# A hybrid attention and recurrence block: two operand slots of the recurrence, and the place of one transposition

## The chip, the cores and the metric

The kernel runs on one core of a Trainium2 chip. The metric is the device time of one execution in microseconds (us). The core has a matrix engine (TensorE, PE in the profile), a vector engine (VectorE, DVE), a scalar engine (ScalarE, ACT), a general engine (GpSimd, POOL) and an engine that here only issues transfers (SyncE, SP). Each works through its own list of instructions; semaphores tie the lists together.

## The reference

One transformer block over a sequence of 1024 tokens and a width of 1024: a projection `w_in` into queries, keys and values of an attention with forget gates (8 heads of 64), into the inputs of an RWKV7 recurrence (8 heads of 64) and into two gates; both branches, their gated sum through `w_o`, and then a convolutional feed-forward part with 2816 channels. The change lies in the recurrence:

```python
def rwkv7_time_mix(p, mu, w0, w2, a0, a2, g2, k_k, k_a, r_k, ln_w, ln_b):
    p = p + (token_shift(p) - p) * mu
    r, k, v, xw, xa, xg = _split(p, RWKV_SPLITS)
    ...
    kk = heads(k * k_k)
    kk = kk / jnp.maximum(jnp.sqrt(jnp.sum(kk * kk, axis=-1, keepdims=True)), L2_EPS)
    k_mod = k.astype(jnp.float32) * (1 + (a - 1) * k_a)
    ...
    def step(state, inp):
        r_t, w_t, k_t, v_t, a_t, b_t = inp
        sa = jnp.einsum('bhvk,bhk->bhv', state, a_t)
        state = state * w_t[:, :, None, :] + sa[..., None] * b_t[:, :, None, :] + v_t[..., None] * k_t[:, :, None, :]
        y_t = jnp.einsum('bhvk,bhk->bhv', state, r_t)
        return state, y_t
    ...
    bonus = (jnp.sum(r_h * k_h * r_k, axis=-1, keepdims=True) * v_h).reshape(bsz, seq, RWKV_WIDTH)
    return ((y + bonus) * g).astype(p.dtype)
```

The last two lines but one hold the bonus: a sum over the 64 channels of each head, times v.

## The kernel before, in words

**Stages.** The program modulates and normalises the input, computes the projections, runs the recurrence with part of the projections between its steps, then the attention, the two output projections, and the feed-forward part. A float32 matmul with the full number of digits is made of three products of rounded parts ("hi" and "lo"): `load_w` loads a block of weights into `raw`, ACT rounds it to hi (line 272), DVE computes lo = raw - hi (line 274).

**The recurrence** works on 8 units: 4 pairs of heads p by 2 halves hf of the sequence, named p_hf (0_0, 0_1, 1_0 and so on to 3_1). A unit has 8 chunks of 64 tokens. In each unit `pre` (from line 697) does what needs no state, and `main` (from line 831) does the rest.

- `pre` loads the log decays into `cum` (line 711) and the rates into `al` (line 713), sums the decays along the chunks with a scan on DVE (line 715, in place), makes `el` and `en` from it with exponentials on ACT (lines 719 and 721), normalises the keys (`ksq`, `rn`, `kr`, lines 723 to 732), forms `ar` and `bk` (lines 737 to 744) and the product `rkb` for the bonus (line 748, in the slot of ksq). Matmuls give the chunk matrices `E` (line 764). Corner blocks of 32 by 32 go to memory and back in another layout (lines 772 and 776), a loop of 31 steps of two small DVE instructions inverts them (lines 784 and 786), and the result returns through memory to `TT` (lines 789 and 797). The transposed v and a are copied to `UV` and `QA` (ACT line 810, DVE line 811), and `q` follows. Then come the bonus sums: `head_sums` (line 825, the function at lines 690 to 696), which rounds its input to a part hi (ACT, line 692), forms the rest lo on POOL (line 693) and adds both over the heads' channels with two matmuls. `bon` (line 827) is the product with v.
- `main` transposes the corner of TT into `X` on DVE (line 842), goes through `xi`, `X` (ACT, line 852), `zi` and back to `TT` (ACT, line 859), `uw`, `mz`, and then a chain through the 8 chunks: a matmul with the state on PE, a scaled copy of it to `S` on ACT (line 903). The normalisation of the output `y` with two more head sums follows (lines 915 to 937).

**Slots.** Most intermediate tiles come from a pool `rw` with one buffer for each tag; `tmp("cum")` takes the buffer tagged cum of width 512 and waits until the tile that had it before has been read for the last time. A tag is used for several tiles in a unit: `ksq` for the squares, for rn, and for rkb; before the change `cum` and `en` are taken again by the two parts of the bonus sums.

**The order.** PE's order is written out by hand: `Weave` (line 48) runs `main` of one unit and `pre` of a later one as two chains of generators, and wherever a chain yields a wait it fills PE with steps of the projections (`rkv_items`, `qk_steps`, `v_steps`, `gate_steps`), by a model of matmul times. The projections leave PSUM through two buffers tagged `big`: `shifted` (lines 354 to 369) scales one copy on ACT (line 366) and evacuates the bank on DVE (line 369); `qk_steps` rounds queries and keys (lines 393 and 395). The orders of DVE, ACT, POOL and SP in this part are chosen by the compiler's scheduler from the dependences and its own costs, except for extra dependences given by hand. Such a dependence of class NOSYNC makes no wait on the chip; it only puts one instruction behind another in a list. `marks` holds instructions for it: the transposition of line 842 goes behind the last `S` copy and the last `E` product recorded at that point.

Of the kernel before, what the change touches and what calls it, by code (L numbers as in the profile page):

```python
# [10 lines left out]
F32R = mybir.dt.float32r  # L11
AF = mybir.ActivationFunctionType
ALU = mybir.AluOpType
# [3 lines left out]
S = 1024  # L17
KT = 8
NH = 512
# [113 lines left out]
def hybrid_block(ctx: ExitStack, tc: tile.TileContext, a, out):  # L133
# [4 lines left out]
    def mm(o, lhsT, rhs, start, stop, more=False):  # L138

        weave.mm_cost(o, lhsT, rhs)  # L140
        nc.tensor.matmul(o, lhsT, rhs, start=start, stop=stop, skip_group_check=more)  # L141
# [5 lines left out]
    def f32(ap):  # L147
        return ap.bitcast(F32)

    tt, stt, ts = nc.vector.tensor_tensor, nc.vector.scalar_tensor_tensor, nc.vector.tensor_scalar  # L150
# [15 lines left out]
    def V(name, i=0, n=1):  # L166
        o, _ = VEC[name]
        return vec[:, o + i : o + i + n]
# [13 lines left out]
    omu = cp.tile([128, 14], F32, name="omu")  # L182
# [61 lines left out]
    marks = {}  # L244
# [40 lines left out]
    def gemm_steps(ps, w, x, cs, nk=KT, w0=0, by_kt=False):  # L285
        (wh, wl), (xh, xl) = w, x
        order = [(i, kt) for i in range(3) for kt in range(nk)]
        if by_kt:
            order.sort(key=lambda o: o[1])
        for n, (i, kt) in enumerate(order):  # L290
            ww, xx = ((wh, xh), (wh, xl), (wl, xh))[i]
            k0 = (w0 + kt) * 128
            mm(ps, ww[:, k0 : k0 + 128], xx[:, kt, cs], start=n == 0, stop=n == len(order) - 1)
            yield
# [51 lines left out]
    with ExitStack() as es:  # L346
# [4 lines left out]
        def big(name):  # L351
            return pb.tile([128, NH], F32, tag="big", name=name)

        def gen(name):
            return pr.tile([128, NH], F32, tag="gen", name=name)

        def shifted(w, ti, hf, dst, prev, name, by_kt=False):

            ps = big(f"ps_{name}{hf}")
            yield from gemm_steps(ps, w, u, slice(hf * NH, hf * NH + NH), by_kt=by_kt)  # L360
            sh = shp.tile([128, NH + 1], F32, tag="sh", name=f"sh_{name}{hf}")
            if hf == 0:
                nc.vector.memset(sh[:, 0:1], 0.0)
            else:
                nc.vector.tensor_copy(sh[:, 0:1], prev)
            nc.scalar.activation(sh[:, 1 : NH + 1], ps, AF.Copy, scale=V("mu", ti))
            if hf == 0:
                nc.gpsimd.tensor_copy(prev, sh[:, NH : NH + 1])
            stt(dst, ps, omu[:, ti : ti + 1], sh[:, 0:NH], op0=ALU.mult, op1=ALU.add)

        rkv, got, last_col = {}, {}, {}

        def rkv_items(p, hf):
            ts_ = {x: rkp.tile([128, NH], F32, tag=f"{x}{hf}", name=f"{x}{p}{hf}") for x in "rkv"}
            rkv[p, hf], got[p, hf] = [ts_[x] for x in "rkv"], 0

            def steps(w, x, t):
                if hf == 0:
                    last_col[p, x] = shp.tile([128, 1], F32, tag=f"pv{x}", name=f"pv{p}{x}")
                yield from shifted(w, t, hf, ts_[x], last_col[p, x], f"rkv{t}")  # L380
                got[p, hf] += 1

            for x, t in (("k", 4 + p), ("r", p), ("v", 8 + p)):
                yield (lambda t=t: w_in(12 + t)), (lambda w, x=x, t=t: steps(w, x, t))
# [305 lines left out]
        def head_sums(ps, x, hi, lo):  # L690

            nc.scalar.copy(hi, x)
            nc.gpsimd.tensor_tensor(lo, x, f32(hi), op=ALU.subtract)
            yield 3400
            mm(ps, blk_r, hi, start=True, stop=False)
            mm(ps, blk_r, lo, start=False, stop=True)

        def pre(k, p, hf):
# [5 lines left out]
            def tmp(nm, w=NH, bufs=1, dt=F32):  # L704
                return rw.tile([128, w], dt, tag=nm, name=f"{nm}{n}", bufs=bufs)

            def chunk_tile(nm, bufs, *dims):
                return rw.tile([128, *dims], F32, tag=nm, name=f"{nm}{n}", bufs=bufs)

            cum = tmp("cum")  # L710
            nc.sync.dma_start(cum, d_lora[0, p, :, cs])
            al = tmp("al")
            nc.sync.dma_start(al, d_lora[1, p, :, cs])
            for c0 in (0, 256):
                nc.vector.tensor_tensor_scan(cum[:, c0 : c0 + 256], cst2[:, 128:384], cum[:, c0 : c0 + 256], initial=0.0,
                                             op0=ALU.mult, op1=ALU.add)
# [3 lines left out]
            en = tmp("en")  # L720
# [10 lines left out]
            kr = tmp("kr")  # L731
# [15 lines left out]
            rkb = tmp("ksq")  # L747
# [6 lines left out]
            E = chunk_tile("E", 2, NCU, 2, 3, CH)  # L754
            QA = chunk_tile("QA", 2, NCU, 2, CH)
            UV = chunk_tile("UV", 2, NCU, 2, CH)
            for c0 in range(0, NCU, 4):
                ps = [gen(f"p1_{n}{h}{c0}") for h in range(2)]
# [54 lines left out]
            ps = [gen(f"tb{n}{h}") for h in range(2)]  # L813
# [8 lines left out]
                    mm(q[HS[h], c * CH : c * CH + CH], E[HS[1 - h], c, h, 0, :], UV[HS[1 - h], c, h, :], start=True, stop=True)  # L822
            nc.vector.tensor_copy(QA[:, :, 0, :], c3(q))
            bp = gen(f"bs{n}")
            yield from head_sums(bp, rkb, tmp("cum", dt=F32R), tmp("en", dt=F32R))
            bon = tmp("bon", bufs=2)
            tt(bon, bp, vv, op=ALU.mult)
            units[p, hf] = dict(ready=ready, pcd=pcd, ar=ar, E=E, QA=QA, TT=TT, bon=bon, UV=UV)
# [1 line left out]
        def main(k, p, hf):  # L830
# [3 lines left out]
            pcd, ar, E, QA, TT, bon, UV = (o[k] for k in ("pcd", "ar", "E", "QA", "TT", "bon", "UV"))  # L834
# [5 lines left out]
            yield max(0, o["ready"] - weave.now - 2500)  # L840
            for h in range(2):
                i = nc.vector.transpose(X[B0[h], :, :], TT[B0[h], :, 0:32])
                for x in ("S", "E"):
                    if x in marks:
                        tc.add_manual_dep(i.ins, marks[x].ins.name, NOSYNC)
            yield max(1300, o["ready"] - weave.now)
# [16 lines left out]
            for c0 in range(0, NCU, 4):  # L863
                ps = gen(f"uw{n}{c0}")
                for c in range(c0, c0 + 4):
                    for h in range(2):
                        x = (c - c0) * 128
# [7 lines left out]
            for c0 in range(0, NCU, 4):  # L875
                ps = gen(f"mz{n}{c0}")
                for c in range(c0, c0 + 4):
                    for h in range(2):
                        x = (c - c0) * 128
# [9 lines left out]
            S = [state.get(p)]  # L889
# [76 lines left out]
        def pre_chain():  # L966
            for k, (p, hf) in enumerate(order):
                while got[p, hf] < 3:
                    yield 200
                yield from pre(k, p, hf)  # L970
                if p < 3:
                    weave.first.extend(rkv_items(p + 1, hf))
                yield 0

        def main_chain():
            for k, (p, hf) in enumerate(order):
                while (p, hf) not in units:
                    yield 200
                yield from main(k, p, hf)
                yield 0  # L980
# [205 lines left out]
    def bank(k, name):  # L1186
        return pb.tile([128, NH], F32, tag="big", name=name) if k > 5 else pz.tile([128, NH], F32, tag=f"p{k}", name=name)
# [125 lines left out]
    for x in range(2):  # L1313
        for n in range(8):
            if x or n:
                k = 8 * x + n + 1
# [313 lines left out]
    ps = {t: [bank(k, f"wo{t}_{c}") for c, k in enumerate(ks)] for t, ks in enumerate(((0, 5), (6, 7), (1, 2)))}  # L1630
# [12 lines left out]
    def wo_do(t, k):  # L1643
        ps = [bank(k + c, f"wo{t}_{c}") for c in range(2)]
        for kt in range(KT):
            wo_mm(t, kt, ps)
        return ps

    ps = wo_do(3, 3)
# [7 lines left out]
    ps = wo_do(4, 0)  # L1657
# [15 lines left out]
    for t, k in ((5, 2), (6, 6), (7, 4)):  # L1673
        ps = wo_do(t, k)
# [229 lines left out]
    for s, k in enumerate(ORDER):  # L1904
        ps = banks[4:] if k in (7, 4, 2) else banks[0:4]
# [109 lines left out]
```

## Time and profile before

| what | value |
|---|---|
| runs, us | 1658.08, 1658.31, 1660.62 (median 1658.31) |
| profiled execution, us | 1662.01 |
| its span, us | 1660.2 |
| mean granted clock of TensorE | 0.989 |
| PE busy, us | 1615.2 (97%) |
| DVE busy, us | 1223.2 (74%) |
| ACT busy, us | 822.3 (50%) |
| POOL busy, us | 130.3 (8%) |
| matmuls | 9694 |

The profile is one execution. A row of the timeline has the start and the duration in us, the engine, the line, the operation, what it writes and reads by the program's names (numbers left out), the shapes, a count of instructions of one kind run together, and in square brackets the idle time of the engine before it with the instruction or transfer that ended this idle time. "SPq" is the issue of a transfer, not the transfer itself. A window's row has the busy us of PE, PE's weight loads, DVE, ACT and POOL, then the granted clock as a share of full speed, the busy share of the transfer engines and the GB/s.

### The profile page before, as it was taken

The numbers are of one execution on the slowest core, as the hardware profiler recorded it, in microseconds if no ns is written. First come the engines' busy times: TensorE is split into PE (matmuls) and PEld (weight loads), VectorE is DVE, ScalarE is ACT, GpSimd is POOL, SyncE is SP. The second block draws the span as 40 slices with busy tenths as digits, with TensorE's granted clock in tenths as the row PEclk, the third lists the DMA queues.
The fourth block names the chain that finished last, engine by engine and source line by source line (L and its number), as shares of the span: only waits on it lengthen the run. The fifth ranks groups of instructions, "written<-read, shape, count | busy, mean of one in ns | idle before, by whom it ended". The sixth has DMA issues, their size and how long they took to land.

```text
span 1660.2 us, 25947 instructions
## 1 busy us (share of the span) xinstructions
PE 1615.2 (97%) x9694; PEld 1346.1 (81%) x9694; DVE 1223.2 (74%) x2371; ACT 822.3 (50%) x1540; POOL 130.3 (8%) x152
## 2 busy tenths in 40 slices
PE   7999999999999999999999999999999999999998
PEld 7777777898978788888778887888888888888886
DVE  5786787878876536888678347897777777786677
ACT  5563335444455656666623225654444444555455
POOL 0011001111111011221022000000000000000000
PEclk9999999999999999999999999999999999999999
DMA  8488645443343246433187411243223223574363
GB/s 336 139 322 238 177 116 140 131 121 97 100 115 97 96 129 153 124 114 110 64 323 265 166 70 58 66 138 108 96 95 120 97 96 108 208 266 156 125 209 108
DMA packets 121645, 240.59 MB, mean 145 GB/s; under 512 B 40048, under 2 KB 48880, under 8 KB 121520
## 3 DMA queue, kind: packets, MB, share of 16 engines
q1 hardware_dynamic: 113040, 220.58, 40.7%
q0 software_dynamic: 8480, 18.37, 4.2%
q8 instruction: 76, 1.25, 0.3%
q14 instruction: 49, 0.40, 0.1%
HBM read 173.35 MB, written 65.54 MB: 144 GB/s over the span
## 4 chain that ended last, share of the span: by engine, by line
PE 62%; DVE 3%; ACT 2%; DMA 1%; issue 1%; SPq 0%; ACTq 0%; DVEq 0%
PE X L141 14%; PE D L141 13%; PE Y L141 7%; PE wo L141 5%; PE br L141 5%; PE gt L141 4%; PE rk_ps L141 4%; PE W L141 3%; PE lg L141 2%; PE ov L141 2%; PE tp L145 2%; DVE nm L1049 1%; DVE P L1059 1%; DMA g<-d_gate 0%; DVE tl L1089 0%
## 5 line engine op out<-in xcount | busy, mean ns | idle before, releaser
L141 PE MATMUL D<-op,op 128*128 128x512 f32 x924 | 209.8, 389 | 0.0
L141 PEld LDWEIGHTS D<-op,op 128*128 128x128 f32 x924 | 173.3, 188 | 36.3 <-DVE op L1252 0.3
L141 PE MATMUL X<-T_m,S 128*128 128x512 f32 x440 | 106.9, 389 | 0.0
L141 PEld LDWEIGHTS X<-T_m,S 128*128 128x128 f32 x440 | 82.5, 188 | 17.5 <-ACT x L1542 0.4
L1251 ACT CAST op<-g 128x512 fp32r<-128x512 f32 x77 | 47.8, 621 | 72.1 <-PE D L141 47.8
L1252 DVE TENSOR_TENSOR op<-g,op 128x512 fp32r<-128x512 f32 x77 | 53.0, 688 | 41.1 <-ACT op L1251 41.1
L1502 DVE SCALAR_TENSOR_TENSOR c<-ab,vec,c 128x512 f32<-128x512 f32 x88 | 65.9, 749 | 18.4 <-ACT c L1505 16.8
L784 DVE TENSOR_TENSOR t<-E,M 128x60 f32<-128x60 f32 (+24 forms) x248 | 56.1, 226 | 26.6 <-DMA M<-sm 20.6
L274 DVE TENSOR_TENSOR lo_in<-raw_in,hi_in 128x512 fp32r<-128x512 f32 x84 | 57.7, 725 | 22.0 <-PE gt L141 7.2
L1466 DVE TENSOR_TENSOR A<-ur,A 128x512 fp32r<-128x512 f32 x64 | 43.9, 688 | 39.0 <-ACT A L1462 38.8
L1466 DVE TENSOR_TENSOR S<-ur,S 128x512 fp32r<-128x512 f32 x66 | 45.5, 691 | 35.2 <-ACT S L1462 35.1
L1462 ACT CAST S<-ur 128x512 fp32r<-128x512 f32 x66 | 41.0, 622 | 56.1 <-DVE ur L1455 30.9
L141 PE MATMUL Y<-T_h,S 128*128 128x512 f32 x264 | 65.6, 398 | 1.6 <-ACT T_h L1720 1.0
L141 PE MATMUL Y<-T_h,A 128*128 128x512 f32 x264 | 63.4, 389 | 0.0
L1053 ACT ACTIVATE P<-lg,nm 128x896 f32<-128x896 f32 (+3 forms) x64 | 47.4, 742 | 29.3 <-DVE nm L1049 19.6
L141 PEld LDWEIGHTS Y<-T_h,S 128*128 128x128 f32 x264 | 50.6, 192 | 13.4 <-ACT T_h L1720 1.8
L1462 ACT CAST A<-ur 128x512 fp32r<-128x512 f32 x64 | 39.6, 621 | 42.9 <-PE X L141 31.0
L141 PE MATMUL W<-B_f,A 128*128 128x512 f32 x252 | 60.6, 389 | 0.0
L786 DVE TENSOR_TENSOR E<-E,t 128x60 f32<-128x60 f32 (+24 forms) x248 | 55.8, 225 | 6.4
L141 PE MATMUL X<-B_b,A 128*128 128x512 f32 x252 | 60.5, 389 | 0.0
L141 PEld LDWEIGHTS Y<-T_h,A 128*128 128x128 f32 x264 | 49.5, 188 | 10.3
L272 ACT CAST hi_in<-raw_in 128x1024 fp32r<-128x1024 f32 x42 | 43.9, 1049 | 25.4 <-PE ps_rkv L141 11.3
(481 smaller groups left out, 4142.0 us busy)
## 6 DMA issues: line engine op xcount, KB each, us to landing
raw_in<-in_w_in SPq DMA_DIRECT2D x50, 512.0 KB, 3.9
wm<-in_w_mod SPq DMA_DIRECT2D x48, 512.0 KB, 6.7
ur<-in_w_up SPq DMA_DIRECT2D x44, 512.0 KB, 4.0
g<-d_g SPq DMA_DIRECT2D x35, 512.0 KB, 3.8
d_g<-gs SPq DMA_DIRECT2D x44, 256.0 KB, 2.0
d_g<-c SPq DMA_DIRECT2D x33, 256.0 KB, 4.3
d_st<-qh SPq DMA_DIRECT2D x64, 128.0 KB, 2.4
stA<-d_st POOLq DMA_DIRECT2D x8, 1024.0 KB, 6.2
```

The costliest lines, as they stand in the source:

```text
L141: nc.tensor.matmul(o, lhsT, rhs, start=start, stop=stop, skip_group_check=more)
L145: nc.tensor.transpose(o, i, eye)
L272: nc.scalar.copy(hi, raw)
L274: nc.vector.tensor_tensor(lo[:, c : c + NH], raw[:, c : c + NH], f32(hi[:, c : c + NH]), op=ALU.subtract)
L784: tt(tv, E32[:, 0:J, s : s + 1].to_broadcast([128, J, W]), M32[:, s : s + 1, s + 1 : 32].to_broadcast([128, J, W]), op=ALU.mult)
L786: tt(E32[:, 0:J, s + 1 : 32], E32[:, 0:J, s + 1 : 32], tv, op=ALU.add)
L1053: nc.scalar.activation(e[:, 0:n], lg[:, 0:n], AF.Exp, bias=nm[:, 0:1], accum_out=nm[:, 1:2])
L1251: nc.scalar.copy(hi, src)
L1252: tt(lo, src, f32(hi), op=ALU.subtract)
L1462: nc.scalar.copy(hi, src)
L1466: tt(lo, src, f32(hi), op=ALU.subtract)
L1502: stt(c, ab[:, x + hf * NH : x + hf * NH + NH], V("conv_w", 22 * x + i), c, op0=ALU.mult, op1=ALU.add)
```

## The change

The bonus sums' two parts are taken from the slots of `kr` and `al` of the same unit in place of `cum` and `en`. And the evacuation of `shifted` (line 369) is recorded as `marks["bank"]`; the transposition of line 842 in the first unit (k == 0) is put behind the last one so recorded, beside S and E.

```diff
@@ -366,7 +366,7 @@
             nc.scalar.activation(sh[:, 1 : NH + 1], ps, AF.Copy, scale=V("mu", ti))
             if hf == 0:
                 nc.gpsimd.tensor_copy(prev, sh[:, NH : NH + 1])
-            stt(dst, ps, omu[:, ti : ti + 1], sh[:, 0:NH], op0=ALU.mult, op1=ALU.add)
+            marks["bank"] = stt(dst, ps, omu[:, ti : ti + 1], sh[:, 0:NH], op0=ALU.mult, op1=ALU.add)
 
         rkv, got, last_col = {}, {}, {}
 
@@ -822,7 +822,7 @@
                     mm(q[HS[h], c * CH : c * CH + CH], E[HS[1 - h], c, h, 0, :], UV[HS[1 - h], c, h, :], start=True, stop=True)
             nc.vector.tensor_copy(QA[:, :, 0, :], c3(q))
             bp = gen(f"bs{n}")
-            yield from head_sums(bp, rkb, tmp("cum", dt=F32R), tmp("en", dt=F32R))
+            yield from head_sums(bp, rkb, tmp("kr", dt=F32R), tmp("al", dt=F32R))
             bon = tmp("bon", bufs=2)
             tt(bon, bp, vv, op=ALU.mult)
             units[p, hf] = dict(ready=ready, pcd=pcd, ar=ar, E=E, QA=QA, TT=TT, bon=bon, UV=UV)
@@ -840,7 +840,7 @@
             yield max(0, o["ready"] - weave.now - 2500)
             for h in range(2):
                 i = nc.vector.transpose(X[B0[h], :, :], TT[B0[h], :, 0:32])
-                for x in ("S", "E"):
+                for x in ("S", "E", "bank") if k == 0 else ("S", "E"):
                     if x in marks:
                         tc.add_manual_dep(i.ins, marks[x].ins.name, NOSYNC)
             yield max(1300, o["ready"] - weave.now)
```

## The prediction

> **What bounds the kernel now.** I read the profile from the whole to the place: first the busy times, then the table of TensorE's waits, then one-microsecond windows and the timeline around the two largest waits near the change.
>
> ```profile
> span 1660.2 us, 25947 instructions
> PE 1615.2 (97%) x9694; PEld 1346.1 (81%) x9694; DVE 1223.2 (74%) x2371; ACT 822.3 (50%) x1540; POOL 130.3 (8%) x152
> ```
>
> PE is busy for 1615.2 of 1660.2 us. Only 45 us are idle, so a change that adds no matmul and removes none can win only what PE waits near it, and the stretches in which PE's clock is low. The profiled execution took 1662.01 us with a span of 1660.2; the runs' median is 1658.31. I sum in the profiled execution's time and carry the difference over to the median. A measurement of this kernel can tell about 0.2% from no change, 3.3 us here: faster means below 1655.0, slower above 1661.6.
>
> The table of PE's waits (line waited at, releaser: us in total, times, longest) has these rows from the recurrence:
>
> ```profile
> PE uw L141 <- ACT TT L859: 2.9, 2, 2.0
> PE qk L141 <- DVE v L369: 2.7, 1, 2.7
> PE v L141 <- DVE vs L955: 1.9, 3, 1.3
> PE br L141 <- DVE mg_m L1306: 1.9, 1, 1.9
> PE sp L141 <- ACT S L903: 1.1, 1, 1.1
> PE qk L141 <- DVE ql L395: 0.7, 1, 0.7
> PE va L141 <- POOL Wts L693: 0.4, 1, 0.4
> ```
>
> (The br row lies after the recurrence; it serves for comparison below.) The eight units together have about 10.7 us of PE waits, and two of them make up 4.8: qk on line 369 and uw on line 859. Both are followed by a low clock. The windows have busy us by engine, then the granted clock, DMA share and GB/s:
>
> ```profile
> 224.00:225.00 1.00, 0.34 (x1) 0.34 (x2) 0.71 (x2) 0.00 (x0) 0.00 (x0) 0.84 0.70 199
> 228.00:229.00 1.00, 1.00 (x20) 0.60 (x20) 0.86 (x5) 1.00 (x3) 0.00 (x0) 0.96 0.00 0
> 286.00:287.00 1.00, 1.00 (x15) 1.00 (x10) 1.00 (x4) 0.24 (x1) 0.00 (x0) 0.56 0.94 381
> 289.00:290.00 1.00, 1.00 (x5) 0.81 (x4) 0.89 (x5) 0.73 (x2) 0.00 (x0) 0.74 0.19 70
> ```
>
> A mean of 0.84 is 0.68 us at full clock and 0.32 at half: the clock halves at 224.68, and 0.96 puts its return at 228.08. In the same way 0.56 and 0.74 give 286.12 to 289.52. Each stretch lasts 3.4 us at half clock and loses 1.7 us of PE's work. The starts are 61.44 us apart, 18 times 3.41, as if the clock were decided on a fixed grid of 3.41 us: then a gap counts by how much of one grid interval it fills.
>
> **First part: the transposition of unit 0_0.** Timeline around the first wait:
>
> ```profile
> 221.75 0.43 DVE L842 STREAM_TRANSPOSE X<-TT 32x256 f32<-32x256 f32 x1 [4.97 <-DMA TT<-se]
> 222.12 1.24 DVE L274 TENSOR_TENSOR lo_in<-raw_in,hi_in 128x512 fp32r<-128x512 f32 x2
> 223.86 0.75 DVE L369 SCALAR_TENSOR_TENSOR v<-ps_rkv,omu,sh_rkv 128x512 f32<-128x512 f32 x1
> 224.66 1.22 PE L141 MATMUL qk<-u_hi,hi_in 128*128 128x512 f32 x2 [2.75 <-DVE v L369]
> 225.06 0.69 DVE L715 TENSOR_TENSOR_SCAN cum<-cst,cum 128x256 f32<-128x256 f32 x1 [0.36 <-DMA cum<-d_lora]
> ```
>
> DVE stands at X for 4.97 us until TT has come from memory. Behind X in its list stand lo_in and the evacuation of v, which frees the PSUM bank for qk. In the changed program's list both stand ahead of X. The evacuation's inputs were long ready, so PE's 2.75 us vanish, and with them the 1.7 us of half clock: 4.45. X itself comes about 0.16 later, and what is late next is the loop of unit 0_1 behind it.
>
> **Second part: other slots.** The number of instructions is unchanged on every engine; the sums' two parts have the same shapes in the new slots. What moves is when slots are free. cum's slot is now free after the en exponential, not after the bonus matmul, so SP takes the next unit's cum load (line 711) some 25 to 80 us sooner, and the scan, el and en move with it: the scans leave the loop stretch of DVE's list, and el and en leave the place ahead of the TT copies for places within the S copies of line 903. al's load (line 713) goes the other way, into cum's former place; line 737 onward needs it only much later. kr now also waits for the bonus matmul, which is always earlier on PE: nothing, as long as PE's order stands (it does).
>
> ```profile
> 281.77 1.27 DVE L715 TENSOR_TENSOR_SCAN cum<-cst,cum 128x256 f32<-128x256 f32 x2 [1.67 <-DMA cum<-d_lora]
> 283.08 0.63 ACT L719 ACTIVATE el<-cum 128x512 f32<-128x512 f32 x1 [4.00 <-DVE cum L715]
> 283.62 0.61 ACT L721 ACTIVATE en<-cum 128x512 f32<-128x512 f32 x1
> 284.14 0.73 ACT L859 COPY TT<-zi 32x256 f32<-32x256 f32 x2
> 284.54 0.43 PE L141 MATMUL uw<-QA,TT 64*64 64x128 f32 x2 [2.05 <-ACT TT L859]
> ```
>
> Here the TT copy waits behind en, en behind el, el 4.00 us for the scan, the scan 1.67 for its load. With scan, el and en gone from ahead of it the copy follows its own matmul zi, and PE gains 2.05 plus the second 1.7: 3.75. The other uw wait goes the same way (0.9), as does va (0.4). Of the 1.9 on vs, which DVE releases, I count 1.1: DVE has a scan of 1.27 less there, but other work in front of it stays. Gains: 4.45 + 3.75 + 0.9 + 0.4 + 1.1 = 10.6.
>
> **What is given back.** First, where the early scans go:
>
> ```profile
> L715 DVE TENSOR_TENSOR_SCAN cum<-cst,cum 128x256 f32<-128x256 f32 x16 | 10.3, 676 | 8.0 <-DMA cum<-d_lora 7.3 <-PE zi L141 0.7
> ```
>
> Sixteen scans stood 7.3 us for their loads. In the first two units loads are still late and the scan now stands ahead of ql (line 395) and of unit 0_0's loop. Between nothing and one scan with its mean stall (1.27 + 1.0 = 2.27) I take 0.75, a stall of that mean less a little cover; the 0.7 wait on ql grows by it.
>
> Second, DVE has little slack after 222 (first the window from 225 to 254):
>
> ```profile
> 225.00:254.00 29.00, 29.00 (x281) 23.38 (x281) 27.00 (x87) 13.08 (x25) 2.11 (x5) 0.95 0.43 116
> ...
> 249.30 0.75 DVE L369 SCALAR_TENSOR_TENSOR k<-ps_rkv,omu,sh_rkv 128x512 f32<-128x512 f32 x1
> 250.94 0.62 PE L141 MATMUL ps_rkv<-u_hi,hi_in 128*128 128x512 f32 x2
> 252.63 0.31 ACT L903 ACTIVATE S<-sp,pcd 128x64 f32<-128x64 f32 x1
> 253.00 0.42 PE L141 MATMUL sp<-S,Mt 128*128 128x64 f32 x2
> ```
>
> PE would come to 250.94 at 247.2 (4.45 less 0.75 earlier). But it needs the bank that k's evacuation frees, and DVE is busy for 27.0 of these 29 us; its list has become shorter only by the scan, its 0.36 stall and some 0.3, less two loop operations put ahead (0.4) and the 0.16: about 1.3. The evacuation ends near 248.75 instead of 250.05, and PE waits some 1.6 to 1.9. Two microseconds on, the S copy stands in ACT's list behind en of unit 1_1, which needs bk's last reader on DVE (line 744); S comes about 0.85 sooner than before, so PE waits another 1.3 at 253.00. Of 3.7 gained, 0.85 is left: 2.85 given back. Bounds: 1 (all cover holds up to 253) and 3.7.
>
> Third, unit 2_0's en stands ahead of the S copy of 300.32:
>
> ```profile
> 299.91 0.69 DVE L744 TENSOR_TENSOR bk<-al,en 128x512 f32<-128x512 f32 x1
> 300.32 0.31 ACT L903 ACTIVATE S<-sp,pcd 128x64 f32<-128x64 f32 x1
> 301.08 0.33 PE L141 MATMUL sp<-S,Mt 128*128 128x64 f32 x2
> ```
>
> en may start only when this bk is written, at 300.60 less the DVE's earliness of some 3.4; en (0.61), the cast behind it and S follow, and the matmul, now 4.6 early, waits about 1.7. Between 0 (bk comes as early as PE) and 3.0. At unit 3_1 the same costs 0.35.
>
> Fourth, unit 2_1's X, at 466.17, now stands ahead of unit 3_0's four QA copies:
>
> ```profile
> 462.52 1.73 DVE L811 COPY QA<-at 64x256 f32<-64x256 f32 x4 [2.32 <-PE at L145]
> 464.04 2.24 SPq L797 DMA_DIRECT2D TT<-se  x4
> 465.36 1.15 PE L141 MATMUL q<-UV,E 64*64 64x64 f32 x32
> 466.17 0.43 DVE L842 STREAM_TRANSPOSE X<-TT 32x256 f32<-32x256 f32 x1 [1.92 <-DMA TT<-se]
> ```
>
> By then all chains are 3.5 early, and TT's loads pass three stores on SP, so X starts near 462.3; with 0.43 of its own and 1.73 of copies the bank of q is free at 464.5. PE stands there at 465.36 - 3.5 = 461.9, hence about 2.4 of waiting; nothing if the bank were free in time, 3.5 at most before all is returned.
>
> Sum: 10.6 - (0.75 + 2.85 + 1.7 + 0.35 + 2.4) = 2.55 gained.
>
> **The clock in the new gaps.** Gaps of 2.75 and 2.05 were each followed by a half-clock stretch; 1.9 (the br row) was not, nor 1.3 on vs. Of the new gaps one (2.4) lies above this border, but its estimate spans it. I count half a stretch, 0.85, with bounds 0 and three stretches, 5.1. Forecast: -2.55 + 0.85 = -1.7; the profiled execution 1660.3, the median 1658.31 - 1.7 = 1656.6.
>
> The Trainium skill, page "TensorE: Matmul & The Clock Gate", section "Why this matters for your kernels", asks for no idle gaps over about 3 us between bursts of matmuls, since one window of idle returns the clock to half. By that rule no new gap costs clock, and the sum would be -2.55, a median of 1655.8. This trace disagrees: gaps of 2.75 and 2.05 were enough.
>
> **The rivals.** *The gain holds*: DVE and ACT keep pace with PE, and the 2.85, 1.7 and 2.4 are hidden; 10.6 - 1.1 = 9.5 at most, with half of these hidden 6 to 8, so about 1651. For it: S chains have fillers between their steps, so a late S need not stop PE. Against it: DVE is 93% busy in the window from 225 to 254, so it can't follow PE there. *Slower, by en ahead of S in every unit*: en waits for line 744, S copies stand behind it on ACT, sp behind them on PE. I find it uncovered at units 1_1, 2_0 and 3_1. Were it so in five more places at 1.7 each, -2.55 + 8.5 = +5.95: 1664.3. It decides from the fourth such place on (-2.55 + 6.8 = +4.25). Against it: before, the whole recurrence shows only one wait on S, of 1.1. *Nothing*: the freed slot isn't used sooner, since SP's order binds the cum load, or later waits swallow all: 1658.3. Against it: the transposition's move alone is firm, and 0.85 of it survives.
>
> **How the numbers follow.** Forecast 0.55 (own range 1653.5 to 1660, from 1.0 to 3.7 in the second term, 0 to 3.0 in the third and 0 to 5.1 of clock, not all at one end); gain holds 0.20; slower 0.15; nothing 0.10. Faster by over 0.2%: 0.38 of the forecast's 0.55 lies below 1655.0, and nearly all of the gain case: 0.21 + 0.19 = 0.40. Slower: 0.13 of the third case and 0.05 of the others: 0.18. Within: 0.42. Range 1651 to 1661.5, which leaves out the far half of the gain case and most of the slower one.
>
> **What would show it.** Right: no wait of qk on line 369 near 222 and full clock there; no uw wait near 282; new PE waits near 251 to 253 on line 369 and S, near 301 on S, near 465 on the QA copies. Wrong: these are absent and the recurrence ends 6 us or more earlier; or S waits appear in most units. I would also be wrong if PE's busy time itself moved by more than the clock explains.

## The result, and the profile after

| comparison | changed, median us | before, median us | ratio to before (95% interval) |
|---|---|---|---|
| the two kernels, 18 runs each | 1655.6 (1650.98 to 1658.38) | 1658.19 (1655.99 to 1664.01) | 0.9980 (0.9971 to 0.9988) |
| changed, second time (e7) | 1655.07 | 1660.48 | 0.9967 (0.9956 to 0.9979) |
| changed, third time (e11) | 1655.02 | 1661.31 | 0.9963 (0.9949 to 0.9976) |

The forecast was 1656.6, a gain of 1.7 us. The kernel is faster by 0.2 to 0.4%: by 2.6 us in the first comparison, at the border between "within 0.2%" and "faster", and by 5.4 and 6.3 us in the two later ones, which lie beyond it. The profiled execution took 1650.98 us, the shortest of the 18, and the profiled one of before, with 1662.01, was longer than all but two of its 18 runs. The two profiles are 11 us apart where the medians are 2.6 apart: what follows takes the places from the profiles and the size from the runs.

The page of the changed kernel, span and busy times:

```profile
span 1649.2 us, 25947 instructions
PE 1607.7 (97%) x9694; PEld 1340.7 (81%) x9694; DVE 1221.3 (74%) x2371; ACT 823.7 (50%) x1540; POOL 128.3 (8%) x152
```

PE's busy time fell by 7.5 us with the same 9694 matmuls, DVE's and ACT's hardly moved. Most of that is clock: ahead of the stretch at the end of the program, which both have, the before profile has nine grid intervals of 3.41 us at half clock, this one five, and four times 1.7 us is 6.8.

PE's waits of 1.8 us and more in the changed kernel, from the recurrence on (line waited at, releaser: total, times, longest):

```profile
PE q L141 <- DVE QA L811: 2.5, 1, 2.5
PE rk_ps L141 <- ACT gm L1163: 2.3, 3, 1.2
PE br L141 <- DVE mg_m L1306: 2.1, 1, 2.1
PE sp L141 <- ACT S L903: 2.0, 3, 1.0
PE ov L141 <- DVE o L1122: 2.0, 1, 2.0
PE br L141 <- ACT hi_br L1214: 1.8, 1, 1.8
PE qk L141 <- DVE ql L395: 1.8, 1, 1.8
```

Gone are qk on line 369 (2.7), uw on line 859 (2.9), v on vs (1.9), va on Wts (0.4). New are q on QA (2.5) and the growth of qk on ql (0.7 to 1.8) and sp on S (1.1 to 2.0). The timeline of the changed kernel at the places that the prediction named, DVE and ACT first:

```profile
219.65 0.74 DVE L369 SCALAR_TENSOR_TENSOR v<-ps_rkv,omu,sh_rkv 128x512 f32<-128x512 f32 x1
221.18 0.43 DVE L842 STREAM_TRANSPOSE X<-TT 32x256 f32<-32x256 f32 x1 [0.78 <-DMA TT<-se]
247.01 0.75 DVE L369 SCALAR_TENSOR_TENSOR k<-ps_rkv,omu,sh_rkv 128x512 f32<-128x512 f32 x1
...
278.20 0.75 ACT L859 COPY TT<-zi 32x256 f32<-32x256 f32 x2 [1.44 <-PE zi L141]
295.45 0.63 ACT L721 ACTIVATE en<-cum 128x512 f32<-128x512 f32 x1 [0.21 <-DVE bk L744]
295.99 0.30 ACT L903 ACTIVATE S<-sp,pcd 128x64 f32<-128x64 f32 x1
...
458.21 0.43 DVE L842 STREAM_TRANSPOSE X<-TT 32x256 f32<-32x256 f32 x1 [5.51 <-DMA TT<-se]
458.58 1.69 DVE L811 COPY QA<-at 64x256 f32<-64x256 f32 x4
```

v's evacuation is done before X; the TT copy at 278.20 follows its own matmul zi instead of an exponential; S at 295.99 stands behind en, which stands behind bk; and the QA copies at 458.58 stand behind an X for which DVE waited 5.51 us. PE at these and a few more places:

```profile
188.74 0.50 PE L141 MATMUL qk<-u_hi,hi_in 128*128 128x512 f32 x1 [1.81 <-DVE ql L395]
195.90 0.61 PE L141 MATMUL ps_rkv<-u_hi,hi_in 128*128 128x512 f32 x2
226.48 0.69 PE L141 MATMUL xi<-X,E 32*32 32x32 f32 x32
251.13 0.43 PE L141 MATMUL sp<-S,Mt 128*128 128x64 f32 x2 [0.22 <-ACT S L903]
280.58 1.96 PE L141 MATMUL uw<-QA,TT 64*64 64x128 f32 x32
285.92 0.33 PE L141 MATMUL mz<-E,Wt 64*64 64x128 f32 x2
296.33 0.43 PE L141 MATMUL sp<-S,Mt 128*128 128x64 f32 x2 [0.97 <-ACT S L903]
440.80 0.43 PE L141 MATMUL sp<-S,Mt 128*128 128x64 f32 x2
460.41 1.15 PE L141 MATMUL q<-UV,E 64*64 64x64 f32 x32 [2.49 <-DVE QA L811]
538.29 0.32 PE L141 MATMUL sp<-S,Mt 128*128 128x64 f32 x1 [0.83 <-ACT S L903]
```

The same matmuls in the profile of before:

```profile
193.50 0.40 PE L141 MATMUL ps_rkv<-u_hi,hi_in 128*128 128x512 f32 x1
228.74 0.69 PE L141 MATMUL xi<-X,E 32*32 32x32 f32 x32
291.79 0.33 PE L141 MATMUL mz<-E,Wt 64*64 64x128 f32 x2
447.98 0.33 PE L141 MATMUL sp<-S,Mt 128*128 128x64 f32 x2
546.49 0.32 PE L141 MATMUL sp<-S,Mt 128*128 128x64 f32 x1 [1.12 <-ACT S L903]
```

Start after minus start before gives PE's shift: +2.40 at ps_rkv, -2.26 at xi, -1.87 at the sp of 251, -3.96 at uw, -5.87 at mz, -4.75 at the sp of 296, -7.18 at the sp of 440, -4.95 at q, -8.20 at the last. Ahead of ql it was -0.3. Each step between two of these is one term of the sum, below.

### The profile page after: what moved, and what is told of

Its sections match the earlier page's. It is cut to its first block, busy times and chain, and to the rows that moved or that the text cites. A ratio compares the mean times of both kernels' runs of the same rounds, so it can differ in the third digit from the quotient of the medians.

```text
span 1649.2 us, 25947 instructions
## 1 busy us (share of the span) xinstructions
PE 1607.7 (97%) x9694; PEld 1340.7 (81%) x9694; DVE 1221.3 (74%) x2371; ACT 823.7 (50%) x1540; POOL 128.3 (8%) x152
## 4 chain that ended last, share of the span: by engine, by line
PE 62%; DVE 3%; ACT 2%; DMA 1%; issue 1%; SPq 0%; ACTq 0%; DVEq 0%
PE X L141 14%; PE D L141 13%; PE Y L141 7%; PE wo L141 5%; PE br L141 5%; PE gt L141 4%; PE rk_ps L141 4%; PE W L141 3%; PE lg L141 2%; PE ov L141 2%; PE tp L145 2%; DVE nm L1049 1%; DVE P L1059 1%; DMA g<-d_gate 1%; DVE tl L1089 0%
```

## The experiments

Ratios are to the kernel before on the same chip, with 95% intervals.

**Each part alone.** e1 has only the diff's second hunk (kr and al), e2 only the first and third (the mark).

> The slots of kr and al alone, without the mark for the transposition. My theory (the two parts gain at separate places, and each gives back later): PE's wait of 2.7 us on the evacuation of line 369 near 222 stays, the wait of uw on TT near 282 is gone, the new wait of q on the QA copies (2.5 in the changed kernel) and the one of qk on ql (1.8) are there. Time: the changed kernel's median 1655.6 plus 2.7 and up to 1.7 of clock, less what the later waits take back of it: 1657.5 to 1660, no faster than before (1658.2). Rival (the slots carry the whole gain, the transposition's stall is made up further on): 1655 to 1656.

> The mark for the transposition alone, the sums' parts in cum and en as before. My theory: the 2.7 wait near 222 is gone and with it up to 1.7 of clock, uw's wait on TT near 282 stays at 2.0 or grows, because its scan waits for a load that comes no earlier than PE's bonus matmul; no wait of q on QA copies. Time 1655 to 1657, that is 1 to 3 us faster than before. Rival (DVE is the limit after 222, so that k's evacuation and the S copies give it all back by 254): 1658, and new PE waits of 1.5 or more between 245 and 254.

e1: 1657.54 us, 0.9983 (0.9968 to 0.9999). The wait near 222 stayed (2.5), uw's was gone, q waited 2.8 and ql 2.0, as the theory had it. The time did not come as expected: the kernel before had 1660.88 on this chip, so e1 is 0.2% faster where I had expected no gain, and its ratio can't be told from the changed kernel's 0.9980 to 0.9963. What the mark adds to the slots therefore shows in the traces alone: xi starts at 229.10 in e1, and at 226.48, 227.36 and 226.98 in the three profiles of the changed kernel.

e2: 1662.26 us, 1.0013 (0.9997 to 1.0028): no gain, perhaps a loss. Neither the theory nor the rival had the reason. The timeline of e2:

```profile
222.48 0.37 SPq L711 DMA_DIRECT2D cum<-d_lora  x1
227.87 1.27 DVE L715 TENSOR_TENSOR_SCAN cum<-cst,cum 128x256 f32<-128x256 f32 x2 [3.06 <-DMA cum<-d_lora]
229.17 0.63 ACT L719 ACTIVATE el<-cum 128x512 f32<-128x512 f32 x1 [12.23 <-DVE cum L715]
231.93 0.75 ACT L852 COPY X<-xi 32x256 f32<-32x256 f32 x2
232.34 0.86 PE L141 MATMUL zi<-TT,X 32*32 32x32 f32 x12 [4.41 <-ACT X L852]
```

The 2.7 us at qk are gone, but the X copy stands on ACT behind el and en of unit 1_0, these behind a scan, and the scan waited for a load that SP issues only at 222.48. PE stood 4.41 us at zi instead, and two half-clock intervals followed. Read from the bottom up, every row waits for the row above it; X waits for its place on ACT, behind el and the en that follows it.

**How much of the slots the mark needs.** e6 is e2 with the new slots for unit 0_1 only:

```diff
-            yield from head_sums(bp, rkb, tmp("cum", dt=F32R), tmp("en", dt=F32R))
+            yield from head_sums(bp, rkb, tmp("kr" if k == 1 else "cum", dt=F32R),
+                                  tmp("al" if k == 1 else "en", dt=F32R))
```

> The mark for the transposition, and the new slots in the bonus sums of unit 0_1 alone; all other units keep cum and en. In the run with the mark alone PE stood 4.4 us at zi, because the X copy (line 852) was behind el and en of unit 1_0 on ACT, and these behind a scan whose load had come late. My theory (that one unit's slot is what the mark needs): the wait of zi on X and the wait near 222 are both gone, uw's wait of 2.0 near 284 stays, no wait on QA; the ratio to before 0.996 to 0.999. Rival (the late load was an accident of that run, or the X copy waits for something else): the zi wait stays at 3 or more, the ratio is 1.000 to 1.003.

Both waits were gone and uw's stayed (1.7): that one slot is what the mark needs to take them away. The ratio missed: 1.0006 (0.9995 to 1.0016). The scheduler put the freed scan between unit 0_1's kr and bk, and PE waited 1.65 for bk near 199, with a half-clock interval behind it. So no run shows in time what the mark is worth.

**Taking back what was given back.** e3 keeps the transposition of unit 2_1 behind the QA copies, e4 keeps every scan behind the E products, e5 joins e3 with scans behind the QA copies.

```diff
-                    nc.vector.tensor_copy(QA[HS[h], e::2, 1, :], a4[HS[e], :, h, :])
+                    marks["QA"] = nc.vector.tensor_copy(QA[HS[h], e::2, 1, :], a4[HS[e], :, h, :])
...
-                for x in ("S", "E", "bank") if k == 0 else ("S", "E"):
+                for x in ("S", "E", "bank") if k == 0 else ("S", "E", "QA") if k == 5 else ("S", "E"):
```

> The changed kernel with the transposition of unit 2_1 kept behind unit 3_0's four QA copies by a dependence without a wait. My theory (the 2.5 us of q on QA are given back there and nowhere covered): this wait is gone, and the median falls by 1.5 to 2.5 below the changed kernel's 1655.6, to 1653 to 1654. Rival (xi, zi or uw of unit 2_1, which come after X, take over the wait, so that nothing is won): 1655 to 1656 with a new wait on X or TT of about 2 near 463 to 475.

e3: 1653.8 us, 0.9958 (0.9944 to 0.9972). q's wait is gone, but the rival is right in part: va (0.7) and zi (0.6) took over half of it, and from ahead of q to the end of the recurrence PE wins only 0.5 us against the first profile of the changed kernel. The changed kernel did not run on this chip; its ratios of 0.9980 to 0.9963 lie above, and the intervals overlap.

```diff
-                nc.vector.tensor_tensor_scan(cum[:, c0 : c0 + 256], cst2[:, 128:384], cum[:, c0 : c0 + 256], initial=0.0,
+                i = nc.vector.tensor_tensor_scan(cum[:, c0 : c0 + 256], cst2[:, 128:384], cum[:, c0 : c0 + 256], initial=0.0,
                                              op0=ALU.mult, op1=ALU.add)
+                if "E" in marks:
+                    tc.add_manual_dep(i.ins, marks["E"].ins.name, NOSYNC)
```

> The changed kernel with the scans of line 715 kept behind the E products of the unit before, so that they fall into the stretch in which DVE waits for the corner blocks; el and en then also stand behind the S copies. My theory: the wait of qk on ql (1.8, with its half-clock stretch) falls to at most 0.7, and the waits on S near 251 and 296 (1.2 together) vanish; the wait of q on QA stays or grows by up to 1.3, since the last scan now stands ahead of X there. Time 1652.5 to 1655. Rival (the scans' loads are late wherever the scans stand, and DVE loses the same): 1655 to 1657, with the ql wait at 1.5 or more, or new waits on QA or E of the same size.

e4: 1659.22 us, 0.9987 (0.9972 to 1.0002). ql fell to 0.7 as expected, but the scans now stood ahead of QA copies in several units, and q waited three times, 6.1 us in all: the rival's new waits on QA, larger than either side had them. I had priced this at 1.3 for one unit.

> The changed kernel with both the transposition of unit 2_1 and the scans of line 715 kept behind the latest QA copies. My theory (of what the change gives back, the wait of qk on ql and the waits on S come from scans and exponentials taken too soon, and q's wait from copies that stand behind something): no wait of q on QA above 0.5, ql at most 0.8, S together below 1.0; the median against its runs of before at 0.993 to 0.995. Rival (the scan in the gap of DVE delays the loop or el and en ahead of the X copies of line 852, so that another wait appears): 0.996 to 0.998, with a PE wait of 1 or more on X, TT or E.

e5 (the dependence on the last QA copy in place of E): 1656.17 us, 0.9974 (0.9962 to 0.9987). q and ql are quiet; the rival's kind of wait came, at another tile: the scan of unit 3_1 stands on DVE ahead of y (462.98), its el and en on ACT ahead of the cast that the variance sums need (464.29), and PE waited 2.6 at va, with three half-clock intervals behind it. qk also waited 1.3 for the evacuation of v near 222 again.

**One scan.** e9 moves only the scan of unit 1_0 (k == 2) behind unit 0_0's QA copies, with e3's dependence; e10 also puts the en of unit 2_0 (k == 4) behind the last S copy; e12 is e9 again.

```diff
+                if k == 2:
+                    tc.add_manual_dep(i.ins, marks["QA", 0].ins.name, NOSYNC)
```

> The changed kernel with the transposition of unit 2_1 behind the QA copies, as in the third run, and besides one scan moved: that of unit 1_0 (line 715, third of the eight) behind unit 0_0's QA copies, where DVE waits some 6 us for the corner blocks; all other lists as they were. My theory: this one scan, standing 2.9 us for its load ahead of ql and E, is what the wait of qk on ql (1.8 to 2.3) grew by; it falls to 0.5 to 1.0, without a half-clock stretch behind it, and PE at 226 is 1.2 to 2.9 us earlier than in the third run (which stood at 227.1 for xi). Ratio to before 0.993 to 0.996. Rival (the earlier PE only waits longer further on, at S, on the evacuation of line 369 or on va): 0.996 to 0.998, with new waits of 1.2 or more between 226 and 300.

e9: 1651.83 us, 0.9948 (0.9931 to 0.9965). DVE in e9 (its line 813 is line 811 of the changed kernel):

```profile
171.02 1.73 DVE L813 COPY QA<-at 64x256 f32<-64x256 f32 x4 [1.51 <-PE at L145]
172.78 1.27 DVE L715 TENSOR_TENSOR_SCAN cum<-cst,cum 128x256 f32<-128x256 f32 x2
174.09 0.69 DVE L395 SCALAR_TENSOR_TENSOR ql<-qk,qh 128x512 fp32r<-128x512 f32 x1
```

And its PE waits in the recurrence that answer to ql and q:

```profile
PE sp L141 <- ACT S L905: 3.2, 4, 1.4
PE qk L141 <- DVE ql L395: 0.8, 1, 0.8
PE ps_rkv L141 <- DVE k L369: 0.7, 1, 0.7
```

The scan finds its load there (no idle time before it), ql's wait is back at 0.8 without a half-clock interval, and of q's only 0.4 is left, on UV. But most of what PE wins there it loses again: near 250 it waits 0.67 for the evacuation of k and 0.84 for S (0.72 and 0.83 in e12), the rival's places, so that from ahead of ql to the sp near 253 it wins 0.9 us more than in e3, and 0.6 in e12. In the changed kernel the same scan stood for its load ahead of ql, E and the loop of unit 0_0:

```profile
168.50 1.27 DVE L715 TENSOR_TENSOR_SCAN cum<-cst,cum 128x256 f32<-128x256 f32 x2 [2.87 <-DMA cum<-d_lora]
```

> The kernel of the run beside it, and the en exponential of unit 2_0 behind the last S copy of unit 0_1. My theory: PE's wait on S near 296 (1.0 to 1.4) is gone, other waits stay; ratio lower by 0.0005 to 0.001 than the run beside it. Rival (en comes too late for the users of unit 2_0, or the chain's next step waits in place of this one): ratio the same or higher, with a wait of 1 or more at another place between 296 and 350.

e10: 1656.97 us, 0.9972 (0.9959 to 0.9985), 5.1 us above e9 on the same chip. The long S wait at 296 was gone, but the one dependence also moved a scan: the scheduler put unit 2_1's between the E products of unit 1_1.

```profile
310.99 1.28 DVE L715 TENSOR_TENSOR_SCAN cum<-cst,cum 128x256 f32<-128x256 f32 x2 [7.42 <-DMA cum<-d_lora]
312.18 1.26 DVE L768 TENSOR_TENSOR E<-p,cst 128x512 f32<-128x512 f32 x2
```

DVE stood 7.42 us for that load, and PE 2.4 for the E products behind it, with a half-clock interval after it. So e10 doesn't tell what en alone would bring.

> The best version so far (one scan moved, and the transposition of unit 2_1 behind the QA copies) once more, since its first interval, 0.9931 to 0.9965, overlaps the changed kernel's. My theory (3 to 4 us below the changed kernel, from the waits of ql and q): ratio to before 0.993 to 0.9965, no wait on ql above 1.0 and none on QA above 0.5. Rival (the first result was a lucky set of clock phases): 0.9965 to 0.998.

e12: 1652.88 us, 0.9952 (0.9936 to 0.9967), with ql at 0.7 and no wait on QA. e9's version is 0.5% faster than the kernel before, and 3.2 us below the changed kernel's median (e11) on the same chip; the intervals of e9 and e12 still overlap that of e11, and that of e3 too, so that the scan's own share is not shown in time.

**Second profiles.**

> The changed kernel once more, on the chip of the two others. Theory (the waits belong to the program, but which gap is followed by half a clock depends on where a grid of 3.41 us falls in an execution): PE's waits of 1.5 us and more (ql 1.8, q 2.5) come back within 0.5, all half-clock stretches start at one phase of 3.41 us, and this phase and the list of stretches differ from the first profile's. Ratio to before 0.997 to 0.999. Rival (the gaps alone decide the clock): the same four places at half clock as in the first profile.

> The kernel before once more, for a second profile. Theory: the waits of 2.7 near 222 and 2.0 near 282 come back, but not both must be followed by a half-clock stretch; the number of stretches differs from the first profile's by one or more, and the span by about 1.7 us for each. Rival: the same seven places, and a span within 1 us of 1660.2 at the same clock of 0.989.

> The changed kernel on the chip of these two, as their measure: ratio to before 0.997 to 0.998; waits of 2.3 to 2.5 at q and 1.8 to 2.0 at ql once more, half-clock stretches again at one phase of 3.41 us, among places that differ from both earlier profiles by at least one.

The waits came back: ql 1.8, 1.9, 1.6 and q 2.5, 2.3, 2.4 in the three profiles of the changed kernel; 3.0 near 224 and 2.1 near 287 in the second one of before. The half-clock stretches came back in part. Those near 43, 930 and 1025 are in all three profiles of the changed kernel; the one behind ql is in the first and in e7, the one behind q in e7 alone. In e8 both gaps were followed by half clock again, the one near 224 by three intervals. e8 took 1665.81 us with ten half-clock intervals where the first profile had nine; the one interval more is 1.7 of the 3.8 us between them.

## Why the prediction was right, and where it was wrong

The median lies 1.0 us below the forecast, inside its range, but the sum behind it is not as good as that. e7 and e11 moved by 5.4 and 6.3 us where the sum had 1.7, so the closeness of the first comparison is in part luck. By the sum's own steps, with PE's shifts of the three profiles of the changed kernel against the first one of before (it ran 3.8 us above the median of its runs, so these sums may come out too large):

| term | forecast | first profile | e7 | e11 |
|---|---|---|---|---|
| early scans, at ql | +0.75 | +2.7 | +2.8 | +0.95 |
| wait and clock near 222 | -4.45 | -4.66 | -4.65 | -4.2 |
| 251 to 253, DVE without slack | +2.85 | +0.4 | +0.4 | +2.1 |
| uw near 282 and its clock | -3.75 | -4.0 | -4.0 | -4.0 |
| S near 301 | +1.7 | +1.1 | +1.6 | +1.6 |
| vs, with the small term of unit 3_1 | -0.75 | -2.4 | -2.2 | -2.0 |
| q on QA | +2.4 | +2.2 | +2.1 | +2.2 |
| va, uw, and what else follows q | -1.3 | -3.25 | -1.75 | -3.25 |
| sum | -2.55 | -7.9 | -5.8 | -6.6 |

- *Near 222*: the size was right, the reason incomplete. I wrote that the loop of unit 0_1 is late next. In e2 it is the X copy behind el and en: without the slot of unit 0_1 the mark gained nothing. The two parts were summed as if independent, which holds only with both.
- *uw near 282*: right in mechanism and size; e1 has it without the mark.
- *ql*: the mechanism was right (a scan stands for its load ahead of ql), the size too small. The scan's own row in the changed kernel has 2.87 us of idle time and not the group's mean of 1.0. The wait grew by 0.9 to 1.1, and in the first profile and e7 half clock added 1.6. e9 takes this back, and pays for most of it in the next step.
- *251 to 253*: absent in the first profile and e7, present in e11. In the first profile k's evacuation came at 247.01, that is 2.29 earlier, where I had worked out 1.3; and PE came only 2.26 earlier where I had 3.7, because ql had cost more. So they met almost without a wait (0.22). The missing part of DVE's gain: the loop of unit 0_1 began earlier, at 223.64 and not 224.53, which I had put 0.16 later. In e11, with no half clock behind ql, PE comes sooner, counted from ahead of ql, and stands at both places that the prediction named:

```profile
250.03 0.74 PE L141 MATMUL ps_rkv<-u_hi,hi_in 128*128 128x512 f32 x2 [0.68 <-DVE k L369]
253.34 0.43 PE L141 MATMUL sp<-S,Mt 128*128 128x64 f32 x2 [0.84 <-ACT S L903]
```

So this term and ql's are not two: they cost 3.1, 3.1 and 3.0 together in the three profiles, where the sum had 3.6. What PE loses at ql it does not wait for again here.

- *S near 301*: the place and releaser were right; 0.97, 1.41 and 1.40 in the three profiles, where I had 1.7.
- *q on QA*: right, 2.5, 2.3 and 2.4.
- *The clock*: I counted half a stretch for the new gaps. In the three profiles of the changed kernel ql's gap was followed by one in two and q's in one, so it belongs in the range. The border that I drew between 1.9 and 2.05 us does not hold: ql's 1.81 lay within one grid interval and was followed by half clock, the 1.86 of br was split 1.57 and 0.28 and was not.
- *After 301*: here the sum was most wrong, by 3.6 in the first profile and 3.2 in e11. In the first profile vs gives its whole 1.7 where I counted 1.1, a step near 380 gives 0.7 that I did not have, the 0.35 of unit 3_1 does not come, and behind q there are steps of 0.6 at va, 1.0 at zi and 1.4 at uw where I counted 0.4, nothing and 0.9. That DVE's list is shorter by a scan in every unit there fits this; no run shows it by itself.

The rest of the 11 us between the first two profiles is clock in the attention and later, where the change does nothing. Of the rivals, "the gain holds" fits the first pair of profiles (8.2 us by the end of the recurrence, beyond the 6 that the prediction named as a sign of being wrong) and not the first comparison's medians; "slower" did not come: S waits stayed at three or four places.

## What to carry to other kernels

A buffer that frees sooner lets a scheduler move the whole producer chain, and an early consumer of a late load at the head of an engine's list can cost more than a late one (2.87 us here, 7.42 in e10): look for the instruction that stands for its load and ask what is behind it. Pin that one instruction, and not its whole class: with X behind the QA copies in each, all scans pinned gave 0.9974, one scan pinned 0.9948 and 0.9952, and none 0.9958. The step from none to one is within the noise. When a wait is removed, ask for the last releaser of each following step, since here the second one (el and en ahead of the X copy) was hidden by the first.

## What the runs showed of the hardware

The granted clock is decided on a grid of about 3.41 us whose phase differs from execution to execution. Two windows of the changed kernel's first profile and two of its second (e7), in which the clock falls to half within the window; the clock is the last number but two:

```profile
189.00:190.00 1.00, 1.00 (x5) 0.83 (x5) 0.86 (x5) 0.36 (x1) 0.00 (x0) 0.88 0.19 45
927.00:928.00 1.00, 1.00 (x4) 0.79 (x3) 0.00 (x0) 0.00 (x0) 0.00 (x0) 0.52 0.00 0
```

```profile
190.00:191.00 1.00, 1.00 (x4) 0.76 (x3) 0.86 (x5) 0.20 (x1) 0.00 (x0) 0.56 0.36 84
927.00:928.00 1.00, 1.00 (x8) 1.00 (x9) 0.17 (x1) 0.00 (x0) 0.00 (x0) 0.70 0.07 29
```

The starts are 189.76 and 927.04 in the first, 190.12 and 927.40 in the second: 737.28 us apart in both, 216 times 3.4133. In all 14 profiles every stretch starts on one such grid and lasts 3.4, 6.8 or 10.2 us, but for the last one, which runs into the end of the program.

PE's wait of 1.97 to 1.98 us for o (line 1122 in the table of waits above), far behind the change, is the same in all 14 profiles and so a test of what decides. Lay the grid through the starts of a profile's stretches: in the six profiles in which 1.95 to 1.98 us of the gap fell into one interval, the next interval was at half clock; in the eight in which it was split, with 1.83 or less in one interval, none was. This is not all there is: a gap with 1.84 us in one interval near 831 was followed by half clock in e2, one with 1.65 near 199 in e6, and one with 1.90 near 844 was not in e12, so what PE does in the rest of the interval must count too; that stays open.

Nor is it idle time alone. In twelve of the 14 profiles a stretch starts between 927 and 943 with no gap of PE in the interval before it. What stands there are 32 matmuls of a single column, which the profile counts as busy; in the changed kernel's first profile:

```profile
922.73 3.63 PE L141 MATMUL mps<-cst,acc 128*128 128x1 f32 x32
```

In these twelve 2.06 to 2.74 us of them fell into one interval, and the next one was at half clock; in e1 and e9 they were split, with 1.83 or less in each, and it was not. That is close to the border for idle time, as if such matmuls hardly counted as activity.

The Trainium skill, page "TensorE: Matmul & The Clock Gate", section "What's actually happening" and the table in "Why this matters for your kernels", has a free-running window of 4096 cycles, some 3.4 us, and advises against idle gaps over about 3 us. The grid agrees with the window; the limit doesn't: 1.98 us were enough where they fell into one interval.

The mean clock also goes with much of the spread between executions: among the 18 runs of the changed kernel the four with a mean clock of 0.994 or more took 1651.33 to 1654.64 us, the three at 0.990 took 1657.13 to 1658.38. The shortest, 1650.98, had 0.993, so the clock is not all of it.
